# Two modulation vectors of each FFN phase as row sums on the vector engine, and six raw buffers instead of seven

## The chip, the cores and the metric

One core of a Trainium2 chip runs the kernel. The metric is the device time of one execution in microseconds (us). Times within one execution are counted from the first instruction of its profile. A change of 0.2% of this kernel is 2.75 us.

## What is computed

The reference is a trunk of two layers. Each layer is run for 128 context tokens and 128 latent tokens with the same weights. A layer has three parts (a gated FFN, a token mixer, a second gated FFN), and each part is modulated by a shift, a scale and a gate that come from the conditioning vector of the token group:

```python
def modulate(x, shift, scale):
    return x * (1 + scale[:, None, :]) + shift[:, None, :]
def adaln(cvec, w, b):                        # w: (1024, 9 * 1024), b: (9 * 1024,)
    m = jax.nn.silu(cvec) @ w + b
    return jnp.split(m, N_MOD, axis=-1)
...
    sh1, sc1, gt1, sh2, sc2, gt2, sh3, sc3, gt3 = mods
    u = modulate(rms_norm(x, g[0]), sh1, sc1)
    x = x + 0.5 * gt1[:, None, :] * swiglu(u, lp['w_ffn1_in'], lp['w_ffn1_out'])
    u = modulate(rms_norm(x, g[1]), sh2, sc2)
    y, ctx_out = token_mixer(u, lp, lam_init, ctx)
    x = x + gt2[:, None, :] * y
    u = modulate(rms_norm(x, g[2]), sh3, sc3)
    x = x + 0.5 * gt3[:, None, :] * swiglu(u, lp['w_ffn2_in'], lp['w_ffn2_out'])
```

`adaln` gives nine vectors of 1024 values for each layer and for each of two conditioning vectors. Each of the nine reads a 1024 x 1024 slice of `w_ada`, 4 MB in float32. `DEPTH` is 2, so there are 18 such vectors; vector (l, m) is number m of layer l.

## The kernel before, in words

All weights come from HBM in float32 and are used once. A weight chunk (`Chunk`, mostly 1 MB, 8 KB in each partition) is loaded by the SP queue into one of `N_RAW` = 7 buffers named `raw` (L1466 to L1471). Its products need float32 accuracy, so each half of a chunk (a `Unit`) is split by `split_one` into a rounded part `whi` (scalar engine, L1493) and a remainder `wlo` (vector engine, L1494). `mm3` (L167) then multiplies three pairs of parts on the tensor engine: high by high (L168), high by low (L169) and low by high (L170). Six split units may wait for the tensor engine (`N_SPLIT`). A raw buffer is given back when the last reader of its chunk is through, and `pump_dma` then lets SP issue the next chunk of one fixed list. That list is sorted by need: a chunk that is split is due six units ahead of its products, a chunk that is read as it is stands at its own step.

The program is a list of steps, worked off in order by the executor at the end of the file; each engine sees its own instructions in that order. An FFN's first part has eleven column pairs of four units (24 matmuls each), its second part has 24 units. The FFN phases begin at 0, 507, 708 and 1175 us, and their first parts end at about 175, 645, 845 and 1305 us. The mixers lie between them.

The modulation vectors that a later part needs are worked out as extra steps, which `spread_into` puts evenly between the steps of a phase. `ADA` says which vectors each phase works out, and in which of two ways:

- A vector of the second list takes four 1 MB chunks of `w_ada`, two at a time in one step. `side` (L310) runs 16 instructions of the tensor engine with 512 columns for two chunks: four products side by side, each with 32 columns of `cT` as the stationary operand (`pd<-raw,cT`, L165). So a vector is two steps.
- A vector of the first list is first summed over its eight channel blocks on the vector engine: 28 of 32 instructions multiply a 128 x 512 block by one value per partition and add it to `acc` (L339), the others begin the sum (L337). Then `total` sums the 128 lanes of `acc` on the tensor engine with the constant `hot` (`pd<-acc,hot`), twice for each vector.

At the end of a phase `post` transposes the gathered sums, adds the two halves and the bias, and finishes scale and gate vectors.

Three FFN phases have one vector of the first kind and two of the second, the last FFN phase has one of the first kind. The mixers have three of the second kind each. The first two vectors, (0, 0) and (0, 1), belong to `begin`, the opening of the kernel, in which each 1 MB chunk of `w_ada` gives one channel block (L1343 to L1403). `begin` ends with `last` and then `s_loads` (L257), which loads some small inputs over the POOL queue; the step list of the first phase has its modulation steps from its 20th step on.

Of the kernel before, what the change touches and what calls it, by code (L numbers as in the profile page):

```python
# [17 lines left out]
P = 128  # L18
# [15 lines left out]
N_RAW = 7  # L34
# [5 lines left out]
HOT = 10  # L40
LAG = 2
# modulation vectors that each phase works out: those the vector engine sums first, and the others
ADA = {(0, "ffn1"): ([(0, 4)], [(0, 2), (0, 3)]),
       (0, "mixer"): ([], [(0, 7), (0, 6), (0, 5)]),
       (0, "ffn2"): ([(1, 1)], [(0, 8), (1, 0)]),
       (1, "ffn1"): ([(1, 4)], [(1, 2), (1, 3)]),
# [33 lines left out]
def _pack(inputs):  # L80
    """Short vectors side by side, 128 wide, and the per-head gate biases and stabilisers."""
# [43 lines left out]
def trunk_kernel(ctx: ExitStack, tc: tile.TileContext, a: dict):  # L125
# [18 lines left out]
    def t2(shape, name, dt=F32):  # L144
        return tp.tile(shape, dt, tag="t2", name=name, bufs=N_T2)
# [38 lines left out]
    # ---------------------------------------------------------------- small inputs  # L184
# [15 lines left out]
    hot = const.tile([P, HOT + 32], F32, name="hot")  # L200
    po.memset(hot, 0.0)
    po.memset(hot[:, HOT:HOT + 1], 1.0)
# [4 lines left out]
    # ---------------------------------------------------------------- persistent  # L207
# [9 lines left out]
    identb = const.tile([P, P], BF16, name="identb")  # L217
    maskb = const.tile([P, 2, P], BF16, name="maskb")
# [25 lines left out]
    # ---------------------------------------------------------------- start-up  # L244
# [12 lines left out]
    def s_loads():  # L257
        late_in["msk"] = t2([P, 2, P], "msk")
        late_in["lamp"] = t2([P, DEPTH, 4, 64], "lamp")
        po.dma_start(out=late_in["lamp"], in_=a["attn_lambda"].partition_broadcast(P))  # L260
        po.dma_start(out=cst[:, C_CS:C_MF], in_=a["cst"][:, C_CS:C_MF])
        po.dma_start(out=late_in["msk"], in_=a["cst"][:, C_MF:C_END].rearrange("p (d t) -> p d t", d=2))
# [35 lines left out]
    # ---------------------------------------------------------------- modulation  # L298
    def mod_steps(mods_):
        """Products of some modulation vectors.  # L300

        Four products run side by side: two quarters of the channels, two terms of their sums.
        Vector i takes the rows 2 i and 2 i + 1 of each. The vector engine first sums the channel
        blocks of those of the first list, one term per group, and the products sum its lanes."""
        on_ve, on_pe = mods_
        n_ve, mods_ = len(on_ve), on_ve + on_pe
        st = {"left": 4 * len(on_pe) + 2 * n_ve}
# [12 lines left out]

        for i, (l, m) in enumerate(on_ve):
            for r in range(2):
                acc = []
                for jj in range(2):
                    f0 = m * D + r * 512
                    ch = Chunk(a["w_ada"][l, jj * 512:(jj + 1) * 512, f0:f0 + 512], 4, 512)
                    for e in range(4):
                        u = Unit(ch, e, e + 1, 0, 512, split=False)

                        def fn(u=u, k=4 * jj + e, acc=acc):  # L330
                            w = u.raw()[:, 0, :]
                            if k == 0:
                                acc.append(blk([P, 2, 512], "acc"))
                            for g in range(2):
                                c, x = cT[:, k, CT + g:CT + g + 1], acc[0][:, g, :]
                                if k == 0:
                                    ve.tensor_scalar(x, w, c, None, op0=ALU.mult)  # L337
                                else:
                                    ve.scalar_tensor_tensor(x, w, c, x, op0=ALU.mult, op1=ALU.add)  # L339

                        seq.append(((2 * i + r) * 8 + 4 * jj + e + 0.5, fn, [u]))

                def total(i=i, r=r, acc=acc):
                    side([(hot[:, HOT - 2 * i - g:HOT - 2 * i - g + 32], acc[0][:, g, c * 256:c * 256 + 256])
                          for g in range(2) for c in range(2)], r * 256, r * 256 + 256)

                seq.append(((2 * i + r) * 8 + 7.5 + LAG, total, []))
        span = 16 * n_ve if n_ve else 1
        for i, (l, m) in enumerate(on_pe):
            for j2 in range(2):  # L350
# [5 lines left out]
                def fn(us=us, i=n_ve + i, j2=j2):  # L356
# [5 lines left out]
                seq.append(((4 * i + 2 * j2 + 0.4) * span / (4 * len(on_pe)), fn, us))  # L362
        seq.sort(key=lambda x: x[0])
        out = [x[1:] for x in seq]

        def post():
# [12 lines left out]
            for i, (l, m) in enumerate(mods_):  # L379
                o, x = mods[l, m], full[:, :, 2 * i:2 * i + 2]  # L380
                bT = parT[l][:, m * KD:(m + 1) * KD].unsqueeze(2).to_broadcast([P, KD, 2])
                ve.tensor_add(o, x, bT)
                if m % 3 == 1:
                    k0 = 72 + m // 3 * KD
# [1175 lines left out]
```

## Time and profile before

| | us |
|---|---|
| three runs | 1376.32, 1376.99, 1379.35 |
| median of the runs | 1376.99 |
| the profiled execution, first to last instruction | 1375.88 |
| tensor engine (PE) busy in it | 1351.3 (98%) |
| vector engine (DVE) busy | 915.0 (67%) |
| scalar engine (ACT) busy | 682.3 (50%) |
| moved by DMA | 303.68 MB |

The profile is of one execution. Its record runs from the first to the last instruction, and that span, 1375.88 us, is the only time that the record has of it; it lies 1.1 us under the median of the runs. "Busy" is the time in which at least one instruction of the engine runs. An engine's weight loads (PEld) overlap its matmuls.

### The profile page before, as it was taken

How to read it: one execution, taken by the hardware profiler on the slowest of the kernel's cores; microseconds unless marked ns; L12 is line 12 of the kernel's file. 1: busy time of each engine (PE TensorE's matmuls, PEld its weight loads, DVE VectorE, ACT ScalarE, POOL GpSimd, SP SyncE). 2: the span in 40 equal slices, each digit the busy share in tenths (PEclk: the TensorE clock that was granted, in tenths of full speed). 3: DMA queues.
4: the chain of work that ended last, by engine and by line, in shares of the span. 5: the costliest groups of instructions: out<-in, count | busy, mean ns of one | idle time of the engine just before them, and what ended most of it. 6: DMA issues, size and time to landing. Idle time of an engine off the chain costs nothing.

```text
span 1375.9 us, 26101 instructions
## 1 busy us (share of the span) xinstructions
PE 1351.3 (98%) x10915; PEld 1268.7 (92%) x10916; DVE 915.0 (67%) x1440; ACT 682.3 (50%) x1096; POOL 113.0 (8%) x138
## 2 busy tenths in 40 slices
PE   6999999999999999999999999999999999999998
PEld 4999899888998999999998999998899899999998
DVE  4576755876557589666568666667665668887653
ACT  4544444666544466444455444546564445744442
POOL 2000001300000030000020000130000001200000
PEclk8999999999999999999999999999999999999999
DMA  9999856564468847886639876748445895487520
GB/s 293 333 345 340 260 174 213 159 195 138 157 238 298 272 154 267 300 269 212 206 124 321 305 257 197 204 130 241 154 137 195 297 304 186 147 264 233 192 85 31
DMA packets 247526, 303.68 MB, mean 221 GB/s; under 512 B 5537, under 2 KB 212657, under 8 KB 247409
## 3 DMA queue, kind: packets, MB, share of 16 engines
q1 hardware_dynamic: 245728, 296.98, 66.4%
q0 software_dynamic: 1680, 5.05, 1.1%
q8 instruction: 85, 1.39, 0.4%
q14 instruction: 33, 0.26, 0.1%
HBM read 297.80 MB, written 3.15 MB: 219 GB/s over the span
## 4 chain that ended last, share of the span: by engine, by line
PE 90%; DVE 6%; ACT 2%; DMA 1%; issue 1%; SPq 1%; POOL 0%; ACTq 0%; DVEq 0%
PE pm L168 26%; PE pm L170 25%; PE pm L169 25%; PE pd L165 5%; PE pb L165 2%; DVE wlo L1494 2%; DVE v L498 2%; DVE ul L180 1%; PE pm L752 1%; PE pm L754 1%; PE pm L753 1%; ACT whi L1493 1%; PE pa L165 1%; DMA raw<-w_ada 1%; PE pa L173 1%
## 5 line engine op out<-in xcount | busy, mean ns | idle before, releaser
L1494 DVE TENSOR_TENSOR wlo<-raw,whi 128x1024 fp32r<-128x1024 f32 (+1 forms) x424 | 507.3, 1204 | 326.4 <-ACT whi L1493 316.8
L1493 ACT CAST whi<-raw 128x1024 fp32r<-128x1024 f32 (+1 forms) x424 | 433.9, 1031 | 364.3 <-PE pm L169 253.4
L168 PE MATMUL pm<-uh,whi 128*128 128x256 f32 x1928 | 554.7, 288 | 0.0
L169 PE MATMUL pm<-ul,whi 128*128 128x256 f32 x1928 | 546.8, 284 | 1.7 <-DVE v L498 1.3
L170 PE MATMUL pm<-uh,wlo 128*128 128x256 f32 x1928 | 544.7, 283 | 3.2 <-DVE wlo L1494 3.2
L168 PEld LDWEIGHTS pm<-uh,whi 128*128 128x128 f32 x1928 | 366.8, 190 | 23.7 <-ACT whi L1493 9.1
L170 PEld LDWEIGHTS pm<-uh,wlo 128*128 128x128 f32 x1928 | 366.4, 190 | 4.4 <-DVE wlo L1494 4.4
L169 PEld LDWEIGHTS pm<-ul,whi 128*128 128x128 f32 x1928 | 366.2, 190 | 3.8 <-DVE v L498 1.7
L169 PE MATMUL pm<-hl,whi 128*128 128x256 f32 x704 | 197.9, 281 | 0.0
L168 PE MATMUL pm<-hh,whi 128*128 128x256 f32 x704 | 197.5, 281 | 0.0
L170 PE MATMUL pm<-hh,wlo 128*128 128x256 f32 x704 | 197.5, 281 | 0.0
L168 PEld LDWEIGHTS pm<-hh,whi 128*128 128x128 f32 x704 | 132.8, 189 | 0.0
L170 PEld LDWEIGHTS pm<-hh,wlo 128*128 128x128 f32 x704 | 132.7, 189 | 0.0
L169 PEld LDWEIGHTS pm<-hl,whi 128*128 128x128 f32 x704 | 132.6, 188 | 0.0
L423 POOL TENSOR_TENSOR nsum<-nsum,nsq 128x256 f32<-128x256 f32 x36 | 36.4, 1012 | 833.7 <-ACT nsq L421 833.7
L339 DVE SCALAR_TENSOR_TENSOR acc<-raw,cT,acc 128x512 f32<-128x512 f32 x112 | 78.9, 746 | 0.0
L165 PE MATMUL pd<-raw,cT 128*32 128x512 f32 (+1 forms) x512 | 56.5, 560 | 8.7 <-DMA raw<-w_ada 5.0
L653 ACT ACTIVATE silu<-pm 128x512 f32<-128x512 f32 x39 | 23.3, 597 | 69.5 <-PE pm L170 69.5
L165 PEld LDWEIGHTS pd<-raw,cT 128*32 128x32 f32 x512 | 14.0, 112 | 30.8 <-issue 20.4
L655 DVE TENSOR_TENSOR silu<-silu,pm 128x512 f32<-128x512 f32 x40 | 27.4, 685 | 22.6 <-PE pm L170 22.6
L568 DVE SCALAR_TENSOR_TENSOR xT<-pm,mod,xT 128x128 f32<-128x128 f32 x96 | 28.8, 342 | 18.1 <-PE pm L170 18.0
L1238 ACT ACTIVATE sig<-pm 128x512 f32<-128x512 f32 x24 | 14.4, 598 | 50.3 <-PE pm L170 50.1
(340 smaller groups left out, 1757.8 us busy)
## 6 DMA issues: line engine op xcount, KB each, us to landing
raw<-w_ffn_in SPq DMA_DIRECT2D x88, 1024.0 KB, 7.1
raw<-w_ada SPq DMA_DIRECT2D x64, 1024.0 KB, 6.0
raw<-w_ffn_out SPq DMA_DIRECT2D x32, 1024.0 KB, 7.1
raw<-w_in SPq DMA_DIRECT2D x32, 1024.0 KB, 5.9
raw<-w_branch_gate SPq DMA_DIRECT2D x24, 1024.0 KB, 5.4
raw<-w_ffn_out SPq DMA_DIRECT2D x16, 768.0 KB, 4.8
raw<-w_ada SPq DMA_DIRECT2D x16, 512.0 KB, 7.3
raw<-w_out SPq DMA_DIRECT2D x8, 1024.0 KB, 6.6
```

Source lines behind the costliest of these rows:

```text
L165: pe.matmul(out, lhsT, rhs, start=start, stop=stop)
L168: pe.matmul(out, sh, mh, start=start, stop=False)
L169: pe.matmul(out, sh, ml, start=False, stop=False)
L170: pe.matmul(out, sl, mh, start=False, stop=stop)
L339: ve.scalar_tensor_tensor(x, w, c, x, op0=ALU.mult, op1=ALU.add)
L423: eng.tensor_add(self.sum, self.sum, sq)
L498: ve.tensor_scalar(v[:, G[1]], v[:, G[1]], self.scale[:, k, 1:2], self.shift[:, k, 1:2], op0=ALU.mult, op1=ALU.add)
L568: ve.scalar_tensor_tensor(xT[:, k, G[g]], ps[:, G[g]], gate[:, k, g:g + 1], xT[:, k, G[g]], op0=ALU.mult, op1=ALU.add)
L653: ac.activation(st["s"], st["a"], AF.Silu)
L655: ve.tensor_mul(st["s"], st["s"], st["g"])
L1493: ac.copy(u.hi, r)
L1494: ve.tensor_sub(u.lo, r, u.hi.bitcast(F32))
```

## The change

The vectors of the first list are worked out in another way, one more vector of three phases moves to that list, and one raw buffer goes.

```diff
-N_RAW = 7
+N_RAW = 6
...
-ADA = {(0, "ffn1"): ([(0, 4)], [(0, 2), (0, 3)]),
+ADA = {(0, "ffn1"): ([(0, 4), (0, 3)], [(0, 2)]),
        (0, "mixer"): ([], [(0, 7), (0, 6), (0, 5)]),
-       (0, "ffn2"): ([(1, 1)], [(0, 8), (1, 0)]),
-       (1, "ffn1"): ([(1, 4)], [(1, 2), (1, 3)]),
+       (0, "ffn2"): ([(1, 1), (1, 0)], [(0, 8)]),
+       (1, "ffn1"): ([(1, 4), (1, 3)], [(1, 2)]),
        (1, "mixer"): ([], [(1, 7), (1, 6), (1, 5)]),
        (1, "ffn2"): ([(1, 8)], [])}
...
+    cb = const.tile([P, 2, D], F32, name="cb")
...
     def s_loads():
...
+        po.dma_start(out=cb, in_=a["cc"].partition_broadcast(P))
+        ac.activation(cb, cb, AF.Silu)
         po.dma_start(out=late_in["lamp"], in_=a["attn_lambda"].partition_broadcast(P))
...
         for i, (l, m) in enumerate(on_ve):
-            for r in range(2):
...
-                                if k == 0:
-                                    ve.tensor_scalar(x, w, c, None, op0=ALU.mult)
-                                else:
-                                    ve.scalar_tensor_tensor(x, w, c, x, op0=ALU.mult, op1=ALU.add)
...
-                def total(i=i, r=r, acc=acc):
-                    side([(hot[:, HOT - 2 * i - g:HOT - 2 * i - g + 32], acc[0][:, g, c * 256:c * 256 + 256])
-                          for g in range(2) for c in range(2)], r * 256, r * 256 + 256)
...
+            o, junk = mods[l, m], []
+            for j in range(KD // 2):
+                ch = Chunk(a["w_adaT"][l, m, j], 2, D)
+                for b in range(2):
+                    for g in range(2):
+                        u = Unit(ch, b, b + 1, 0, D, split=False)
+
+                        def fn(u=u, k=2 * j + b, g=g, o=o, l=l, m=m, junk=junk):
+                            if not junk:
+                                junk.append(blk([P, D], "junkw"))
+                            ve.tensor_tensor_reduce(junk[0], u.raw()[:, 0, :], cb[:, g, :], 1.0, 0.0,
+                                                    op0=ALU.mult, op1=ALU.add, accum_out=o[:, k, g:g + 1])
+                            if k == KD - 1 and g == 1:
+                                finish(l, m, o, o)
+
+                        seq.append(((i + (4 * j + 2 * b + g) / 16) / len(on_ve), fn, [u]))
...
+        if not mods_:
+            return out
...
+    arrays["cc"] = np.stack([inputs["c_ctx"], inputs["c"][0]])
+    wt = inputs["w_ada"].reshape(DEPTH, D, N_MOD, KD // 2, 2, P)
+    arrays["w_adaT"] = np.ascontiguousarray(wt.transpose(0, 2, 3, 5, 4, 1))
```

`w_adaT` is `w_ada` with its output channels along the partitions and its 1024 input channels in a row, two blocks of 128 output channels to a 1 MB chunk, 8 KB in one piece for each partition. The host lays it out. `cb` is the SiLU of both conditioning vectors, the same 2 x 1024 values in every partition (1 MB in all, as large as the raw buffer that goes). One `tensor_tensor_reduce` multiplies a 128 x 1024 block by one of the two vectors and writes the sum of each row, which is the modulation value of that output channel. So a vector of the first list is 16 steps of one vector-engine instruction each, with no product and no `total`; `finish` is the old end of `post` as a function of its own. Where the second list is empty, `post` is left out. The constant `hot` and its memsets are gone.

## Rows read from the trace of the kernel before

**Rows 1.** The page: engine totals, forty equal slices, and the chain that ended last.

```profile
PE 1351.3 (98%) x10915; PEld 1268.7 (92%) x10916; DVE 915.0 (67%) x1440; ACT 682.3 (50%) x1096; POOL 113.0 (8%) x138
...
PE   6999999999999999999999999999999999999998
...
PEclk8999999999999999999999999999999999999999
DMA  9999856564468847886639876748445895487520
...
PE 90%; DVE 6%; ACT 2%; DMA 1%; issue 1%; SPq 1%; POOL 0%; ACTq 0%; DVEq 0%
```

**Rows 2.** Stretches: start:end, length, busy of each engine (instructions), clock, DMA share, GB/s.

```profile
10.00:50.00 40.00, 31.29 (x256) 21.98 (x256) 18.88 (x46) 15.37 (x29) 9.81 (x11) 0.83 1.13 311
80.00:172.00 92.00, 91.21 (x764) 83.27 (x763) 65.03 (x84) 39.81 (x46) 0.00 (x0) 1.00 0.91 307
519.00:644.00 125.00, 124.24 (x1044) 116.47 (x1043) 90.29 (x123) 59.20 (x76) 0.00 (x0) 1.00 0.84 277
1188.00:1305.00 117.00, 116.24 (x984) 114.68 (x983) 89.69 (x121) 59.33 (x76) 0.00 (x0) 1.00 0.69 225
```

**Rows 3.** PE by line: the first three of 519 to 644 us, the last of 80 to 172.

```profile
L165 PE MATMUL pd<-raw,cT 128*32 128x512 f32 x64 | 7.7, 598 | 0.0
L165 PE MATMUL pd<-acc,hot 128*32 128x256 f32 x16 | 1.3, 391 | 0.0
L173 PE MATMUL pd<-cst,adaev 128*128 128x128 f32 x4 | 0.6, 272 | 0.0
...
L165 PE MATMUL pd<-acc,hot 128*32 128x256 f32 x16 | 1.9, 391 | 0.8 <-DVE acc L339 0.8
```

**Rows 4.** DVE by line, 519 to 644 us: busy, mean ns of one, idle before.

```profile
L1494 DVE TENSOR_TENSOR wlo<-raw,whi 128x1024 fp32r<-128x1024 f32 (+1 forms) x44 | 53.0, 1216 | 28.6 <-ACT whi L1493 27.5 <-PE pd L165 1.1
L339 DVE SCALAR_TENSOR_TENSOR acc<-raw,cT,acc 128x512 f32<-128x512 f32 x28 | 19.7, 745 | 0.0
L655 DVE TENSOR_TENSOR silu<-silu,pm 128x512 f32<-128x512 f32 x9 | 6.2, 685 | 5.0 <-PE pm L170 5.0
L337 DVE TENSOR_SCALAR acc<-raw,cT 128x512 f32<-128x512 f32 x4 | 1.8, 482 | 0.0
```

**Rows 5.** Other shapes, whole span, by form: a smaller DVE instruction, the scalar engine's accumulator.

```profile
L865 DVE SCALAR_TENSOR_TENSOR pl<-e,cf,pl 128x256 f32<-128x256 f32 x8 | 3.5, 481 | 0.1
...
L856 ACT ACTIVATION_READ_ACCUMULATOR e<-pa,mx 128x1 f32 x16 | 3.6, 228 | 0.0
```

**Rows 6.** POOL in order of time, 0 to 60 us, the issue of lamp and what precedes it.

```profile
12.84 7.39 POOL L1394 TENSOR_TENSOR v<-xT,bcs 128x256 f32<-128x256 f32 x7 [1.85 <-ACT bcs L486]
44.73 0.63 POOL L260 DMA_DIRECT2D lamp<-attn_lambda  x1 [24.50 <-PE pd L173]
```

**Rows 7.** Who waited for whom, 0 to 60 us: total, times, longest.

```profile
PE pd L165 <- DMA raw<-w_ada: 5.0, 3, 3.5
```

**Rows 8.** The scalar engine in order of time, 52 to 70 us.

```profile
55.98 3.88 ACT L1493 CAST whi<-raw 128x1024 fp32r<-128x1024 f32 x4
...
60.38 2.00 ACT L1493 CAST whi<-raw 128x1024 fp32r<-128x1024 f32 x2
```

**Rows 9.** SP's own waits over the whole span.

```profile
SPq L1471 <- DVE wlo L1494: 864.1, 166, 21.1
```

**Rows 10.** SP issues by time, 519 to 580 us, then the product that reads the pair.

```profile
561.05 6.61 SPq L1471 DMA_DIRECT2D raw<-w_ada  x2
572.43 7.65 SPq L1471 DMA_DIRECT2D raw<-w_ffn_in  x4
...
578.59 1.50 PE L165 MATMUL pd<-raw,cT 128*32 128x512 f32 x12
```

**Rows 11.** DMA issues: KB each, median us to landing; whole span, then 519 to 644.

```profile
raw<-w_ada SPq DMA_DIRECT2D x64, 1024.0 KB, 6.0
...
raw<-w_ada SPq DMA_DIRECT2D x9, 1024.0 KB, 8.5
```

More of the change, by code (lines that the diff above doesn't have):

```diff
@@ L39 @@
 CT = 8
-HOT = 10
-LAG = 2
-ADA = {(0, "ffn1"): ([(0, 4)], [(0, 2), (0, 3)]),
+ADA = {(0, "ffn1"): ([(0, 4), (0, 3)], [(0, 2)]),
        (0, "mixer"): ([], [(0, 7), (0, 6), (0, 5)]),
-       (0, "ffn2"): ([(1, 1)], [(0, 8), (1, 0)]),
-       (1, "ffn1"): ([(1, 4)], [(1, 2), (1, 3)]),
+       (0, "ffn2"): ([(1, 1), (1, 0)], [(0, 8)]),
+       (1, "ffn1"): ([(1, 4), (1, 3)], [(1, 2)]),
        (1, "mixer"): ([], [(1, 7), (1, 6), (1, 5)]),
@@ L199, in trunk_kernel @@
     po.memset(expo, -0.5)
-    hot = const.tile([P, HOT + 32], F32, name="hot")
-    po.memset(hot, 0.0)
-    po.memset(hot[:, HOT:HOT + 1], 1.0)
     cT = const.tile([P, KD, CT + 32], F32, name="cT")
@@ L299, in mod_steps @@
     def mod_steps(mods_):
-        on_ve, on_pe = mods_
-        n_ve, mods_ = len(on_ve), on_ve + on_pe
-        st = {"left": 4 * len(on_pe) + 2 * n_ve}
+        on_ve, mods_ = mods_
+        st = {"left": 4 * len(mods_)}
         seq = []
@@ L319, in side @@
                 ac.copy(st["ev"], st["ps"])
-        for i, (l, m) in enumerate(on_ve):
-            for r in range(2):
[L323 to L331, printed above, removed]
-                            if k == 0:
[L333 to L336, printed above, removed]
-                                    ve.tensor_scalar(x, w, c, None, op0=ALU.mult)
-                                else:
-                                    ve.scalar_tensor_tensor(x, w, c, x, op0=ALU.mult, op1=ALU.add)
-                        seq.append(((2 * i + r) * 8 + 4 * jj + e + 0.5, fn, [u]))
-                def total(i=i, r=r, acc=acc):
-                    side([(hot[:, HOT - 2 * i - g:HOT - 2 * i - g + 32], acc[0][:, g, c * 256:c * 256 + 256])
-                          for g in range(2) for c in range(2)], r * 256, r * 256 + 256)
-                seq.append(((2 * i + r) * 8 + 7.5 + LAG, total, []))
@@ L348, in mod_steps, with finish @@
-        span = 16 * n_ve if n_ve else 1
-        for i, (l, m) in enumerate(on_pe):
+        def finish(l, m, o, x):
+            bT = parT[l][:, m * KD:(m + 1) * KD].unsqueeze(2).to_broadcast([P, KD, 2])
+            ve.tensor_add(o, x, bT)
+            if m % 3 == 1:
+                k0 = 72 + m // 3 * KD
+                gT = parT[l][:, k0:k0 + KD].unsqueeze(2).to_broadcast([P, KD, 2])
+                ve.scalar_tensor_tensor(o, o, 1.0, gT, op0=ALU.add, op1=ALU.mult)
+            elif m % 3 == 2 and m != 5:
+                ve.tensor_scalar(o, o, 0.5, None, op0=ALU.mult)
@@ L350, in mod_steps @@
+        for i, (l, m) in enumerate(mods_):
             for j2 in range(2):
@@ L354, in mod_steps, with fn @@
                     us.append(Unit(ch, 0, 2, 0, D, split=False))
-                def fn(us=us, i=n_ve + i, j2=j2):
+                def fn(us=us, i=i, j2=j2):
                     for j, u in enumerate(us, 2 * j2):
@@ L360, in fn @@
                               for e in range(2) for c in range(2)], 0, 512)
-                seq.append(((4 * i + 2 * j2 + 0.4) * span / (4 * len(on_pe)), fn, us))
+                seq.append(((2 * i + j2 + 0.4) / (2 * len(mods_)), fn, us))
         seq.sort(key=lambda x: x[0])
         out = [x[1:] for x in seq]
+        if not mods_:
+            return out
         def post():
@@ L379, in post @@
             for i, (l, m) in enumerate(mods_):
[L380 to L384, printed above, removed]
-                    gT = parT[l][:, k0:k0 + KD].unsqueeze(2).to_broadcast([P, KD, 2])
-                    ve.scalar_tensor_tensor(o, o, 1.0, gT, op0=ALU.add, op1=ALU.mult)
-                elif m % 3 == 2 and m != 5:
-                    ve.tensor_scalar(o, o, 0.5, None, op0=ALU.mult)
+                finish(l, m, mods[l, m], full[:, :, 2 * i:2 * i + 2])
         out.append((post, []))
@@ L1470, in pump_dma @@
             else:
-                nc.sync.dma_start(out=t, in_=c.src.rearrange("(k p) f -> p k f", p=P))
+                src = c.src if len(c.src.shape) == 3 else c.src.rearrange("(k p) f -> p k f", p=P)
+                nc.sync.dma_start(out=t, in_=src)
             c.tile = t
```

## The prediction

> **What bounds the kernel now.** I read the page first [rows 1]. The tensor engine is busy 98% of the span, all slices but the first and the last are full, its clock is granted nearly everywhere, and the chain that ended last runs through it for 90%. The vector engine has a third of its time free. So an instruction that leaves the tensor engine should shorten the run by its own length, unless something else then ends last. What that could be I read from stretches [rows 2]. From 10 to 50 us, in `begin`, the tensor engine is busy 31.29 of 40 us and the DMA engines are saturated (share 1.13, 311 GB/s): the start is bound by loading. In the first phase's modulation stretch (80 to 172 us) the tensor engine is full, DMA stands at 0.91 and the vector engine at 65.03 of 92 us. In the second FFN phase (519 to 644) DMA is at 0.84, the vector engine at 90.29 of 125; the third repeats it. The last (1188 to 1305) has DMA at 0.69.
>
> **What the change takes from the tensor engine.** In one FFN phase the two vectors of the second list are 64 instructions, 7.7 us together, 3.85 us for each vector [rows 3]. A second price: the stretches 519 to 644 and 1188 to 1305 do the same FFN work with and without two such vectors, and differ by 124.24 - 116.24 = 8.0 us of tensor time [rows 2], 4.0 us for each, with what switching costs. I take 4.0. Three vectors move: 12.0 us. `total` goes in all four phases, 1.3 us in each [rows 3] (in the first the row reads 1.9 because its group is stretched by a wait of 0.8 us for `acc`, which goes too): 5.2 + 0.8 us. In the last phase `post`'s four transposes go: 0.6 us [rows 3]. Sum: 12.0 + 5.2 + 0.8 + 0.6 = **18.6 us**.
>
> **What it puts on the vector engine.** No row shows a `tensor_tensor_reduce`. By the nearest rows: a plain two-input 128x1024 instruction (`wlo`) takes 1.22 us, or 53.0 / 44 = 1.20 us of busy time [rows 4]. `scalar_tensor_tensor` takes 745 ns for 512 columns and 481 ns for 256 [rows 4, 5], so 1.03 ns a column, and 745 + 528 = 1273 ns for 1024. Neighbours overlap a little: 28 of them fill 19.7 us, 0.70 us each and not 0.745 [rows 4], which makes it 1.23 us. Writing the row sum may cost nothing or, as on the scalar engine, an instruction of its own of up to 0.23 us [rows 5]. Bounds 1.2 and 1.46 us; I take 1.3, since the form is nearest to `scalar_tensor_tensor`.
>
> [...]
>
> In the second and third FFN phases the vector engine gives back 19.7 + 1.8 = 21.5 us [rows 4] and gets 32 x 1.3 = 41.6: 90.3 - 21.5 + 41.6 = 110.4 us in a stretch that shrinks to 125 - 8/2 - 1.3 = 119.7 us. It fits, at 92%. In the first phase the same 32 instructions lie in the shorter stretch: 65.0 - 21.5 + 41.6 = 85.1 us in 92 - 4.0 - 1.3 - 0.8 = 85.9 us, 99%. The cover here is the stock of six split units (six times 24 matmuls, some 17 us of products) and the gated products' PSUM tiles (three tiles, which let the vector engine fall four units, about 11 us, behind). The waits for `whi` that the vector engine now has (27.5 us in the second phase [rows 4]) are idle time ahead of a full stock and go first. At 1.46 us the first phase wants 90.2 us: 4.3 us late, inside that cover. The last phase trades 21.5 us for 20.8. So I cost the vector engine at nothing.
>
> **What it adds elsewhere.** (a) `cb` is one more megabyte. Its issue stands in `s_loads`, but on POOL's queue it is next after the seven multiplications that end at 12.84 + 7.39 = 20.2 us; what follows there now, `lamp`, waits 24.5 us for a buffer of its own [rows 6], and `cb`, being a constant tile, needs none. So it lands in the middle of the saturated start, where products already wait for chunks of `w_ada` (5.0 us in three waits [rows 7]). 1.05 MB at 311 GB/s is 3.4 us [rows 2]. Bounds: 0 (hidden behind the other waits of the start) and 3.4; I take 3.4, as the chunks behind it are used as they land. The SiLU of 128 x 2048 on the scalar engine, about twice the 1.04 us of a 1024-column cast, stands at about 60 us between casts [rows 8] that run six units ahead; `cb` has then long landed, so nothing waits. If the cover failed it would cost 2.1 us once.
>
> (b) Six raw buffers. SP waits 864 us in all for a raw buffer that `wlo` frees [rows 9], so the buffers are full most of the time and each issue moves to the next release. In the second FFN phase the second chunk of a pair for the tensor engine is issued at about 567.3, the next release is at 572.4, and the pair is used at 578.6 [rows 10]. Issued at 572.4 it lands at 578.4 by the whole span's median of 6.0 us, or at 580.9 by this stretch's 8.5 [rows 11]: a wait of 0 to 2.3 us for each pair. Six such pairs remain in the FFN phases (twelve before), with fewer loads bunched around them; the mixers' pairs have more room. Bounds 0 and 13.8 us; I take 1.0.
>
> (c) The first phase's loading. 307 GB/s over 92 us is 28.2 MB; at a full share (307 / 0.91 = 337 GB/s) that takes 83.8 us, and the tensor engine will want it in 85.9. DMA is then at 98%, with one buffer fewer to smooth it. Bounds 0 (it keeps up) and 6.1 us (the phase stays as long as it is); I take half, 3.0. The new chunks come in 8 KB pieces instead of 2 and 4 KB, which no row here prices; I give it nothing.
>
> **Sum.** -18.6 + 3.4 + 1.0 + 3.0 = -11.2 us against the span of 1375.9 us; with 1.1 us outside it the median was 1377.0, so I predict **1366 us**. With every added cost at 0 it is 1358.4.
>
> **The rivals.**
>
> 1. *Loading takes most of it.* The start costs 3.4, the first phase gains nothing (6.1), and each pair elsewhere waits 1 us (6): -18.6 + 15.5 = -3.1, 1374 us. For it: share 1.13 at the start and 0.91 after. Against it: the second and third phases load at 0.84 and the last at 0.69 [rows 2].
>
> 2. *Six buffers are too few: slower.* As rival 1, but every pair waits the full 2.3 us: -18.6 + 3.4 + 6.1 + 13.8 = +4.7, 1382 us. The place is `pd<-raw,cT` in the FFN phases, where the tensor engine stands still with its own queue behind it. It turns slower once a pair waits over (18.6 - 9.5) / 6 = 1.5 us. Against it: only half as many pairs are left there.
>
> [...]
>
> 4. *Nothing to measure*, within 0.2% (2.75 us, about what a measurement of this kernel tells from no change): the upper half of rival 1 or the lower edge of rival 2.
>
> **How the numbers follow.** My forecast, 1357 to 1371 us: 0.64. Rival 1 (1371 to 1377): 0.18, two thirds of it still over 0.2% faster. Rival 2: 0.10. Rival 3: 0.07. Over: 0.01. So faster 0.64 + 0.12 = 0.76, the same 0.06 + 0.02 = 0.08, slower 0.16. The range reaches from every added cost at nothing, 1357, to the end of rival 1, 1377.
>
> **What would show it.** Right: `pd<-raw,cT` falls from 64 to 32 instructions in each of three FFN phases and `pd<-acc,hot` is gone; the row sum reads 1.2 to 1.46 us; the stretch of the second FFN phase ends some 5 us sooner after its start; the first chunks of `w_ada` land about 3 us later. Wrong: a row sum of 2 us or more, with idle tensor time released by `wlo` or by the gated products' tiles in the FFN phases; or idle tensor time before `pd<-raw,cT`, released by DMA. If the start is not longer, (a) was hidden; if the first phase is shorter by the full 6 us, (c) was.

## The result: 1361.2 us, 15.4 us less, and the profile after

| | before | after |
|---|---|---|
| median of the runs, us | 1376.65 (4 runs) | 1361.21 (4 runs, 1359.85 to 1361.61) |
| ratio to before, 95% interval | | 0.9889 [0.9875, 0.9904] |
| profiled execution, first to last instruction, us | 1375.9 | 1358.1 |
| PE / DVE busy in it, us | 1351.3 / 915.0 | 1328.9 / 959.8 |

The forecast was 1366 us. The kernel got faster by 15.4 us between the medians and by 17.8 us between the two profiled executions, and both lie beyond the 11.2 us of the sum. The page of the kernel after, with the lines that answer to [rows 1]:

```profile
PE 1328.9 (98%) x10752; PEld 1258.0 (93%) x10752; DVE 959.8 (71%) x1533; ACT 683.0 (50%) x1096; POOL 113.4 (8%) x137
...
PE   6999999999999999999999999999999999999998
...
DMA  9999966563578846987538987648445895477630
...
PE 84%; DVE 8%; DMA 3%; ACT 2%; issue 1%; SPq 0%; POOL 0%; DVEq 0%; ACTq 0%
```

The tensor engine still sets the time: 98% busy, but 22.4 us less of it. 44.8 us more stand on the vector engine, and the slices between the ends show no gap. The stretches that answer to [rows 2], shifted to where the phases now lie (columns as there):

```profile
10.00:50.00 40.00, 30.51 (x234) 20.82 (x235) 17.45 (x40) 14.05 (x26) 9.05 (x10) 0.79 1.10 312
80.00:172.00 92.00, 92.00 (x777) 88.86 (x776) 84.08 (x128) 44.05 (x51) 0.00 (x0) 1.00 0.91 309
512.00:633.00 121.00, 119.40 (x1002) 115.53 (x1000) 106.09 (x156) 59.34 (x77) 0.00 (x0) 1.00 0.85 286
1172.00:1288.00 116.00, 115.25 (x975) 114.66 (x975) 88.77 (x121) 60.25 (x78) 0.07 (x1) 1.00 0.70 228
```

In the first phase's stretch the tensor engine doesn't stand still at all (92.00 of 92.00 us), although DMA is at 0.91 as before and the vector engine has gone from 65 to 84 us. In the second FFN phase the vector engine is busy 106.1 of 121 us (88%).

The second FFN phase by line, first the vector engine (answers to [rows 4]), then the tensor engine (answers to [rows 3]):

```profile
L1485 DVE TENSOR_TENSOR wlo<-raw,whi 128x1024 fp32r<-128x1024 f32 (+1 forms) x44 | 53.3, 1216 | 8.8 <-ACT whi L1484 8.8
L339 DVE CUSTOM_DVE_ANT_0 junkw<-raw,cb 128x1024 f32<-128x1024 f32 x32 | 39.0, 1219 | 0.0
...
L339 DVE DVE_READ_ACCUMULATOR2_ANT mod<- 128x1 f32 x32 | 2.7, 83 | 0.0
```

```profile
L163 PE MATMUL pd<-raw,cT 128*32 128x512 f32 x32 | 4.1, 601 | 0.8 <-DMA raw<-w_ada 0.8
```

A row sum is two instructions on the vector engine, of 1219 ns for the multiplication and 83 ns for reading the accumulator. They are not to be added, because they overlap. In order of time (two row sums that follow each other at the end):

```profile
96.50 1.22 DVE L339 CUSTOM_DVE_ANT_0 junkw<-raw,cb 128x1024 f32<-128x1024 f32 x1
97.65 0.08 DVE L339 DVE_READ_ACCUMULATOR2_ANT mod<- 128x1 f32 x1
97.65 1.22 DVE L1485 TENSOR_TENSOR wlo<-raw,whi 128x1024 fp32r<-128x1024 f32 x1
...
102.21 1.22 DVE L339 CUSTOM_DVE_ANT_0 junkw<-raw,cb 128x1024 f32<-128x1024 f32 x1
...
103.47 1.23 DVE L339 CUSTOM_DVE_ANT_0 junkw<-raw,cb 128x1024 f32<-128x1024 f32 x1
```

Another instruction starts 1.15 us behind the start of a row sum, a second row sum 1.26 us behind it. The busy time of both instructions of L339 together, in the second FFN phase, is 39.25 us for 32 row sums, 1.23 us each:

```profile
512.00:633.00 121.00, 39.25 (x64) 1.00 0.85 286
```

`pd<-raw,cT` has gone from 64 to 32 instructions and `pd<-acc,hot` is gone. The vector engine's idle time ahead of `whi` has gone from 27.5 to 8.8 us: the row sums took the place of waiting.

**Where the 17.8 us went.** I cut both profiled executions at the same products, found in order of time: the first product of each FFN's first part (`pm<-uh,whi`) and of its second part (`pm<-hh,whi`), rounded to 0.1 us. Two of these cuts are the first `uh` product of the second phase, before and after:

```profile
519.00 0.28 PE L168 MATMUL pm<-uh,whi 128*128 128x256 f32 x1
```

```profile
512.03 0.28 PE L166 MATMUL pm<-uh,whi 128*128 128x256 f32 x1
```

| stretch | before, us | after, us | difference | by the sum |
|---|---|---|---|---|
| start, to the products of the eighth `w_ada` chunk | 49.0 | 50.9 | +1.9 | +3.4 |
| from there to the second part of the first FFN | 126.2 | 119.1 | -7.1 | -6.1 + 3.0 |
| second part, and the first mixer | 343.8 | 342.0 | -1.8 | 0 |
| first part of the second FFN | 125.3 | 120.6 | -4.7 | -5.3 |
| its second part | 75.7 | 75.9 | +0.2 | 0 |
| first part of the third FFN | 124.7 | 120.4 | -4.3 | -5.3 |
| its second part, and the second mixer | 343.1 | 343.5 | +0.4 | 0 |
| first part of the last FFN | 116.8 | 114.4 | -2.4 | -1.9 |
| the rest | 71.3 | 71.3 | 0 | 0 |

The sum's 1.0 us for six buffers has no row of its own; it belongs to the first parts. The -1.8 of the first mixer is the clock's: the stretch lies behind an opening, where the tensor engine has short waits, and in the profiled execution of before its clock then fell (stretches of it: columns as in [rows 2], the clock before the last two):

```profile
250.00:254.00 4.00, 3.29 (x25) 2.71 (x23) 3.54 (x7) 2.20 (x7) 4.00 (x6) 1.00 0.44 132
254.00:258.00 4.00, 3.39 (x13) 2.37 (x14) 2.98 (x5) 3.40 (x5) 1.21 (x4) 0.72 0.42 130
258.00:262.00 4.00, 4.00 (x21) 4.00 (x21) 3.89 (x13) 1.21 (x3) 0.00 (x0) 0.50 0.91 258
```

The same place in the execution of after:

```profile
245.00:249.00 4.00, 3.31 (x24) 2.73 (x22) 3.54 (x8) 2.01 (x6) 4.00 (x6) 1.00 0.56 149
249.00:253.00 4.00, 3.10 (x18) 2.14 (x17) 2.98 (x6) 3.25 (x4) 0.88 (x4) 1.00 0.33 114
253.00:257.00 4.00, 4.00 (x35) 3.94 (x34) 3.86 (x14) 1.40 (x4) 0.00 (x0) 1.00 0.97 291
```

After 3.3 and 3.4 busy microseconds of four the clock stands at 0.50, for 21 instructions in 4 us; with 3.3 and 3.1 it stayed at 1.00, for 35. It isn't the change's: a kernel with the engines' work of after (4 KB pieces, below) shows 0.96 from 225 to 310 us where after shows 1.00, takes 344.0 us for the second part and the first mixer, has a span of 1360.3 us, and the same median. Without the 1.8 us the profiled executions differ by 16.0 us, near the 15.4 of the medians.

### The profile page after: what moved, and what is told of

Its sections match the earlier page's. It is cut to its first block, busy times and chain, and to the rows that moved or that the text cites. A ratio compares the mean times of both kernels' runs of the same rounds, so it can differ in the third digit from the quotient of the medians.

```text
span 1358.1 us, 25895 instructions
## 1 busy us (share of the span) xinstructions
PE 1328.9 (98%) x10752; PEld 1258.0 (93%) x10752; DVE 959.8 (71%) x1533; ACT 683.0 (50%) x1096; POOL 113.4 (8%) x137
## 4 chain that ended last, share of the span: by engine, by line
PE 84%; DVE 8%; DMA 3%; ACT 2%; issue 1%; SPq 0%; POOL 0%; DVEq 0%; ACTq 0%
PE pm L166 25%; PE pm L167 24%; PE pm L168 24%; PE pd L163 3%; DVE wlo L1485 3%; PE pb L163 2%; DMA raw<-w_ada 2%; DVE v L488 2%; ACT whi L1484 1%; DVE ul L178 1%; PE pm L742 1%; PE pm L743 1%; PE pm L744 1%; PE pa L163 1%; DVE junkw L339 1%
## 5 line engine op out<-in xcount | busy, mean ns | idle before, releaser
L166 PEld LDWEIGHTS pm<-uh,whi 128*128 128x128 f32 x1928 | 364.4, 189 | 15.8 <-ACT whi L1484 7.7
L339 DVE CUSTOM_DVE_ANT_0 junkw<-raw,cb 128x1024 f32<-128x1024 f32 x112 | 136.5, 1219 | 0.1
L163 PE MATMUL pd<-raw,cT 128*32 128x512 f32 (+1 forms) x416 | 46.0, 559 | 11.4 <-DMA raw<-w_ada 9.6
L177 ACT CAST hh<-silu 128x512 fp32r<-128x512 f32 (+1 forms) x42 | 25.5, 609 | 32.7 <-DVE silu L645 32.7
L1228 ACT ACTIVATE sig<-pm 128x512 f32<-128x512 f32 x24 | 14.3, 598 | 50.2 <-PE pm L168 50.1
L742 PE MATMUL pm<-whi,uh 128*128 128x512 f32 x96 | 39.3, 409 | 0.0
```

Of the source, the lines that this page charges most:

```text
L163: pe.matmul(out, lhsT, rhs, start=start, stop=stop)
L166: pe.matmul(out, sh, mh, start=start, stop=False)
L177: ac.copy(hi, src)
L339: ve.tensor_tensor_reduce(junk[0], u.raw()[:, 0, :], cb[:, g, :], 1.0, 0.0, op0=ALU.mult, op1=ALU.add, accum_out=o[:, k, g:g + 1])
L742: pe.matmul(ps[g], xh[:, G[g]], wh, start=(k == 0), stop=False)
```

## The experiments

Times are medians beside runs of the kernel before on the same chip; ratios are to the kernel before. A ratio is known to some 0.001 to 0.002, which is 1.4 to 2.8 us, so a difference of 3 us between two changed kernels is near what the medians can tell. Stretches are cut as in the table above.

### One part alone: the row sums without a third vector

```diff
-ADA = {(0, "ffn1"): ([(0, 4), (0, 3)], [(0, 2)]),
+ADA = {(0, "ffn1"): ([(0, 4)], [(0, 2), (0, 3)]),
...
-       (0, "ffn2"): ([(1, 1), (1, 0)], [(0, 8)]),
-       (1, "ffn1"): ([(1, 4), (1, 3)], [(1, 2)]),
+       (0, "ffn2"): ([(1, 1)], [(0, 8), (1, 0)]),
+       (1, "ffn1"): ([(1, 4)], [(1, 2), (1, 3)]),
```

> The changed kernel with the lists of the kernel before: one vector of an FFN phase as row sums, two as products. Against the kernel before it takes only the lane totals and the last transposes from the tensor engine (6.6 us) and pays for cb (2 to 3.4 us) and the buffer (1 to 2). My theory (the gain is the tensor work of the three moved vectors): 1372 to 1375 us, some 12 us over the changed kernel. Rival (the gain comes from how the vector engine's vectors are loaded and summed, in longer pieces and with half the instructions): within 3 us of the changed kernel, 1361 to 1364.

1372.45 us, 0.9968 [0.9956, 0.9980], inside the theory's range and far from the rival's. The four phases' stretches of the table are 123.1, 123.7, 123.4 and 114.3 us, so against before the new form by itself (no `total`, in the last phase no transposes) gave 3.1, 1.6, 1.3 and 2.5 us: 8.5, where the sum had 6.6. Against the kernel after, a moved vector is worth 4.0, 3.1 and 3.0 us: 10.1, where the sum had 12.0. Together 18.6 us, the sum's figure, but that is luck: the new form gave 1.9 us more than the sum had, the moved vectors 1.9 less.

The kernel after waits for `w_ada` once in the second and once in the third FFN phase (510 to 640 and 710 to 840 us):

```profile
PE pd L163 <- DMA raw<-w_ada: 0.8, 1, 0.8
```

```profile
PE pd L163 <- DMA raw<-w_ada: 0.7, 1, 0.7
```

With one row-sum vector and the same six buffers there is no such wait in these two phases. So 1.5 of the 1.9 us by which the moved vectors fell short are these waits.

### One part alone: six raw buffers in the kernel before

```diff
-N_RAW = 7
+N_RAW = 6
```

> The kernel before with six raw buffers instead of seven and nothing else. It keeps all twelve pairs of w_ada chunks in the FFN phases, so it is the harder case for a missing buffer. My theory (the buffer costs a short wait at a pair here and there): 0 to 3 us longer, so 1377 to 1380 us, with waits for w_ada in the trace of at most 1 us each. Rival 2 of the prediction (each pair waits some 2.3 us, and the loading of the first phase falls behind): 12 x 2.3 = 28 us and up to 6 more, so 1400 us or over.

1380.86 us, 1.0033 [1.0023, 1.0044]: the seventh buffer is worth 4.3 us there, a little over my theory's 0 to 3 and far from the rival's 28. The tensor engine's waits from 510 to 640 and from 710 to 850 us, each view's first line:

```profile
PE pd L165 <- DMA raw<-w_ada: 2.0, 1, 2.0
```

```profile
PE pd L165 <- DMA raw<-w_ada: 0.9, 1, 0.9
```

With seven buffers there is no such wait in these phases. The waits stand where the sum put them, at the pairs of chunks for the tensor engine, in the second and third FFN phases, whose first parts took 127.5 and 125.7 us (before: 125.3 and 124.7). One of the two is longer than the 1 us that I had expected at most. The first FFN's stretch stayed at 126.2 us and loads as much as before:

```profile
80.00:172.00 92.00, 91.21 (x765) 83.26 (x764) 65.08 (x85) 39.83 (x46) 0.00 (x0) 1.00 0.89 297
```

So one buffer fewer costs nothing in the phase in which I had feared for the loading.

### The megabyte of `cb` later

```diff
-        po.dma_start(out=cb, in_=a["cc"].partition_broadcast(P))
-        ac.activation(cb, cb, AF.Silu)
...
+        po.dma_start(out=cb, in_=a["cc"].partition_broadcast(P))
...
+            if jj == 3 and l == 0 and which == 1:
+                add(lambda: ac.activation(cb, cb, AF.Silu))
```

The load goes behind the last small input of `s_loads`, the SiLU into a step of its own after `begin`, and the first row sum one step later.

> The changed kernel with the load of cb behind the other small loads on the POOL queue (at about 51 us instead of 21) and its SiLU just ahead of the first row sum. My theory (the megabyte lengthens the saturated start by about its own length): 2 to 3.4 us shorter than the changed kernel, 1358 to 1359 us, and the eighth chunk of w_ada is multiplied at about 48 us instead of 50.9. Rival (the start has slack for it): the same as the changed kernel, 1361 us. Second rival (the first phase, with DMA at 0.91, is tighter than the start): up to 3 us longer, 1364 us.

1357.88 us, 0.9859 [0.9842, 0.9876], 3.3 us less than the kernel after. The issue on POOL, in the kernel after and in this one:

```profile
21.04 0.63 POOL L256 DMA_DIRECT2D cb<-cc  x1
46.55 0.56 POOL L258 DMA_DIRECT2D lamp<-attn_lambda  x1 [24.88 <-PE pd L171]
```

```profile
48.38 0.53 POOL L259 DMA_DIRECT2D cb<-cc  x1
```

Each with a product of the start that waits for `w_ada`, after and here:

```profile
34.35 1.93 PE L163 MATMUL pd<-raw,cT 128*32 128x256 f32 x16 [5.16 <-DMA raw<-w_ada]
```

```profile
31.49 1.93 PE L163 MATMUL pd<-raw,cT 128*32 128x256 f32 x16 [4.04 <-DMA raw<-w_ada]
```

`cb` does go out at 21 us, right behind POOL's multiplications, into the saturated start (DMA share 1.10 from 10 to 50 us), and the same product comes 2.9 us sooner without it. It is so in every profiled execution here: this product starts at 33.9 to 34.4 us in the seven with the early load, and at 31.4 to 31.8 us in the six without it. Term (a), 3.4 us, is thus seen as 3.3 us between the medians and as 2.2 us at the eighth chunk's products of these two executions (50.9 and 48.7 us), and it was avoidable. The first phase's stretch stayed at 119.0 us with `cb`'s load in it, so the second rival's tight first phase did not show.

### The pieces of a load: 4 KB instead of 8 KB

```diff
-                ch = Chunk(a["w_adaT"][l, m, j], 2, D)
+                ch = Chunk(a["w_adaT"][l, m, j].rearrange("b p f -> p b f"), 2, D)
...
-    arrays["w_adaT"] = np.ascontiguousarray(wt.transpose(0, 2, 3, 5, 4, 1))
+    arrays["w_adaT"] = np.ascontiguousarray(wt.transpose(0, 2, 3, 4, 5, 1))
```

> The changed kernel with w_adaT laid out so that each partition's 8 KB of a chunk comes in two pieces of 4 KB that lie apart, as the chunks of the products have it, instead of one. Nothing else differs. My prediction gave the longer pieces nothing: then the same as the changed kernel, 1360 to 1362 us. Rival (the longer pieces are why the first phase kept up with its loading): 1 to 3 us longer, in the first phase, with a longer time to landing for w_adaT.

1361.28 us, 0.9886 [0.9869, 0.9902], against 1361.21. The larger pieces give nothing, as the sum had it.

### The row sums twice: how much cover is there

```diff
                             ve.tensor_tensor_reduce(junk[0], u.raw()[:, 0, :], cb[:, g, :], 1.0, 0.0,
                                                     op0=ALU.mult, op1=ALU.add, accum_out=o[:, k, g:g + 1])
+                            ve.tensor_tensor_reduce(junk[0], u.raw()[:, 0, :], cb[:, g, :], 1.0, 0.0,
+                                                    op0=ALU.mult, op1=ALU.add, accum_out=o[:, k, g:g + 1])
```

Each row sum is worked out a second time into the same place, so that at the prediction's 1.3 us it takes 2.6 us of the vector engine.

> [...] By the prediction's working (11 us of cover in each phase): the first phase 126.7 us of vector work in 85.9, 30 late, the second and third 152.0 in 119.7, 21 late each, the last fits: about 72 us longer than the changed kernel, 1433 us. If the vector engine were no bound until much later, or the cover larger (the 17 us of split units), it would be 18 us less, about 1415; if there were no cover at all, 33 more, 1466.

1422.17 us, 1.0329 [1.0312, 1.0345], 61 us over the kernel after, where I had 72. It shows what a vector engine costs that wants twice the time for its row sums. The first phase's stretch took 139.1 us, 20.0 more, and the second and third phases 17.3 and 18.0 more. Its page, a stretch of the first phase, and the whole first part of the second:

```profile
PE 1345.0 (95%) x10752; PEld 1269.8 (90%) x10752; DVE 1093.5 (77%) x1757; ACT 674.9 (48%) x1096; POOL 113.3 (8%) x137
```

```profile
80.00:172.00 92.00, 79.56 (x637) 74.54 (x636) 90.69 (x141) 31.70 (x38) 0.00 (x0) 0.94 0.71 242
535.68:673.60 137.92, 124.27 (x999) 117.19 (x997) 135.39 (x204) 55.44 (x74) 0.00 (x0) 0.95 0.70 235
```

How far the vector engine may fall behind at no cost, its cover, comes out of this. By the prediction's own busy times it wants 85.1 + 41.6 = 126.7 us in the 85.9 of the first phase, 40.8 too many; 20.0 appeared, which leaves 20.8 us of cover, and in the second phase 110.4 + 41.6 - 119.7 - 17.3 = 15.0. But those busy times are too high. The 112 extra row sums added 1093.5 - 959.8 = 133.7 us, 1.19 us each and 38.2 for the 32 of a phase. With the busy times measured in the kernel after, the first phase has 84.1 + 38.2 - 92 - 20.0 = 10.3 us of cover and the second 106.1 + 38.2 - 121 - 17.3 = 6.0. That is an estimate. It lies nearer to the 11 us of the PSUM tiles with which I had worked out the 72 than to the 17 us of the six split units; which of the two stocks makes the cover wasn't tested. In the trace the last row sum ends 11.1 and 5.8 us after the second part's first product, in the kernel after 2.0 and 5.3 us before it.

The tensor engine's longest waits from 510 to 680 us:

```profile
PE pd L163 <- DMA raw<-w_ada: 11.4, 4, 5.4
PE pm L166 <- DVE silu L647: 1.5, 1, 1.5
```

The vector engine is the one that is short of time, 135.4 of 137.9 us, and yet the longest line names DMA, while DMA's share is 0.70 where the kernel after has 0.85. The longest of these four waits is for a load that was issued late (SP's issue, then the product that reads the chunk):

```profile
562.02 0.37 SPq L1464 DMA_DIRECT2D raw<-w_ada  x1
...
567.17 1.08 PE L163 MATMUL pd<-raw,cT 128*32 128x512 f32 x4 [5.39 <-DMA raw<-w_ada]
```

SP issued this load when a row sum (`mod`, L341) had given its raw buffer back, it landed at 567.13, and the product started 0.04 us later. The row sum is a chunk's last reader, a late vector engine gives the buffer back late, and SP has nowhere to load to. Whoever reads the first line alone blames the wrong thing.

### Three vectors in three phases: where the vector engine becomes the bound

```diff
+ADA = {(0, "ffn1"): ([(0, 4), (0, 3), (0, 2)], []),
...
+       (0, "ffn2"): ([(1, 1), (1, 0), (0, 8)], []),
+       (1, "ffn1"): ([(1, 4), (1, 3), (1, 2)], []),
```

> The changed kernel with all three vectors of an FFN phase as row sums, which leaves the tensor engine no modulation work there. It takes 12 us of products, 2 us of transposes and some 2 us of waits from it, and puts 16 x 1.30 = 20.8 us more on the vector engine of three phases: 106.1 + 20.8 = 126.9 us in about 116 in the second and third, 84.1 + 20.8 = 104.9 in about 87 in the first. My theory (the stock of split units and the PSUM tiles let it fall 11 us behind at no cost): only the first phase is late, by 7 us, so 9 us shorter than the changed kernel, about 1352 us. Rival (what does not fit is lost at once): 10.6 + 10.6 + 18 us late, so about 1384 us.

1355.60 us, 0.9849 [0.9835, 0.9862]: 5.6 us less than the kernel after, so the rival's loss did not come, but also not all of the gain. The first parts of the second and third phases became shorter by 6.6 and 6.7 us (114.0, 113.7), and the first whole phase longer by 2.9 (236.0 against 233.1). In the first phase's stretch the vector engine is full and the tensor engine isn't; in the second phase both are:

```profile
80.00:172.00 92.00, 87.61 (x734) 86.89 (x733) 90.05 (x137) 36.82 (x45) 0.00 (x0) 1.00 0.79 271
517.60:631.60 114.00, 114.00 (x963) 114.00 (x962) 112.25 (x165) 52.46 (x69) 0.00 (x0) 1.00 0.80 271
```

And the phase began later. From the end of the phase before to the first `uh` product it took 14.3 and 15.8 us in the second and third phase, where the kernel after takes 12.5 and 12.5. The vector engine at the opening of the second phase, in order of time, here:

```profile
503.22 1.57 DVE L339 CUSTOM_DVE_ANT_0 junkw<-raw,cb 128x1024 f32<-128x1024 f32 x1
504.72 0.08 DVE L339 DVE_READ_ACCUMULATOR2_ANT mod<- 128x1 f32 x1
504.78 2.36 DVE L1485 TENSOR_TENSOR wlo<-raw,whi 128x1024 fp32r<-128x1024 f32 x2
507.06 0.15 DVE L463 TENSOR_SCALAR var<-pb 128x2 f32<-128x2 f32 x1
```

With an empty second list the first row sum falls due ahead of the phase's first own step, and two splits follow it. `var`, with which the norm of the phase goes on, comes at 507.06, 3.8 us after the residual's end at 503.3; in the kernel after it comes 1.6 us behind it (501.13 against 499.5):

```profile
501.13 0.16 DVE L463 TENSOR_SCALAR var<-pb 128x2 f32<-128x2 f32 x1 [1.62 <-PE pb L163]
```

The tensor engine waits there for the norm, in both phases about 2.1 us; in the second:

```profile
508.51 0.68 PE L163 MATMUL pb<-dg,ones 128*128 128x256 f32 x2 [2.09 <-ACT dg L470]
```

In the third phase its clock fell behind that wait (0.64 over 4 us), which is the larger part of what makes 3.3 us there of the 1.8 in the second:

```profile
702.00:706.00 4.00, 4.00 (x25) 4.00 (x24) 3.96 (x6) 2.99 (x8) 3.80 (x5) 0.64 0.23 94
```

In a phase the row sums have cover (10.3 and 6.0 us by the estimate above); at its opening they had none (2.1 us of waiting).

### The same in two phases, one step later

```diff
-        spread_into(p0 + (21 if begun else 0), p1, mods_)
+        spread_into(p0 + (21 if begun else 1), p1, mods_)
```

With the later `cb`, and three row-sum vectors in the second and third phase alone.

> cb loaded late (1357.9 us), three vectors as row sums in the second and third FFN phase, two in the first, and the first row sum of the second to fourth FFN phase one step later, behind the norm's step and not ahead of it. In three_rowsum the first products of the second and third phase took 6.7 us less than in the changed kernel (114.1 and 113.8 us against 120.8 and 120.6), but they began 1.8 and 3.3 us later after the phase before. My theory (the vector engine's 11 us of cover hold, and the late start came from the row sum that stood ahead of the norm): 2 x 6.7 less, 1344 to 1347 us. Rival (the late start is the price of the fuller vector engine wherever the row sums stand): 5 us more, 1349 to 1351.

1350.09 us, 0.9815 [0.9801, 0.9830], 7.8 us less than with the later `cb` alone; that is the rival's figure and not the theory's. The delay at the openings is gone (12.6 and 12.5 us), but the first parts take 115.0 us each, where three vectors in all three phases had 114.0 and 113.7. The only wait of the tensor engine in this stretch is one of 0.8 us for `wlo`, which the kernel after has too and that run lacks. The vector engine is all but full:

```profile
514.00:630.00 116.00, 115.24 (x970) 114.97 (x971) 114.90 (x168) 53.35 (x69) 0.00 (x0) 1.00 0.82 280
```

114.9 of 116 us: a third vector is what these phases still hold. Its last row sum ends 9.3 us after the second part's first product, so the phase already leans on its cover. A fourth wasn't tried.

### Single chunks, and five buffers

The pairs of chunks for the tensor engine were the place where I had looked for waits. This loads and uses them one at a time:

```diff
-            for j2 in range(2):
+            step = 1 if on_ve else 2
+            for j2 in range(4 // step):
...
-                for j in range(2 * j2, 2 * j2 + 2):
+                for j in range(step * j2, step * j2 + step):
```

> The changed kernel with the products of an FFN phase's one vector taken one w_ada chunk at a time, in four steps spread over the phase instead of two steps of two chunks. The number of chunks, products and row sums is the same. My theory (with six buffers a step that needs two landed chunks at once waits for the second): the waits of the tensor engine for w_ada in the second and third FFN phase (some 1 to 1.7 us in each) go, 1.5 to 3 us shorter than the changed kernel, 1358 to 1360 us. Rival (the wait is the saturated loading itself, whatever the order): no shorter, 1361 us or more.

1361.50 us, 0.9890 [0.9876, 0.9905]: no gain. The two waits of the kernel after, of 0.8 and 0.7 us, are gone here. Whether twice as many steps cost what the wait gave back isn't told apart.

```diff
-N_RAW = 6
+N_RAW = 5
```

> The changed kernel with five raw buffers instead of six. [...] In the kernel before the seventh was worth 4.3 us (raw6), all of it in the second and third FFN phase. My theory (with half of the pairs gone the changed kernel has room at six and is past it at five): 3 to 8 us longer, 1364 to 1369 us, as waits for w_ada at the remaining pairs. Rival (the buffers no longer matter to it): within 1.5 us of 1361.

1374.80 us, 0.9993 [0.9984, 1.0001], 13.6 us more than the kernel after and more than either side expected. The waits of the second phase (510 to 640 us) against the 0.8 us of the kernel after:

```profile
PE pd L163 <- DMA raw<-w_ada: 4.0, 3, 2.2
```

Five buffers take nearly the whole gain back. The first FFN phase got 1.5 us longer, the first parts of the second and third 5.0 and 5.1. Over the whole span the tensor engine waits 21.0 us for `w_ada`, in the kernel after 9.6. The clock took a share: it is 0.97 from 540 to 600 us, where after has 1.00. What a seventh buffer beside `cb` would give in the changed kernel wasn't tried.

### A row-sum vector in each mixer, and all together

With the later `cb`:

```diff
-       (0, "mixer"): ([], [(0, 7), (0, 6), (0, 5)]),
+       (0, "mixer"): ([(0, 6)], [(0, 7), (0, 5)]),
...
-       (1, "mixer"): ([], [(1, 7), (1, 6), (1, 5)]),
+       (1, "mixer"): ([(1, 6)], [(1, 7), (1, 5)]),
```

> The changed kernel with cb loaded late (as in cb_late, 1357.9 us) and one of the three vectors of each mixer moved to row sums as well. It takes 2 x 4 us of products from the tensor engine and puts 20.8 us on the vector engine of each mixer, which is 63% busy in the stretch where these steps lie. My theory (a vector moved is worth its products wherever the vector engine has room): 6 to 8 us shorter than cb_late, 1350 to 1352 us. Rival (the mixers' many short steps on the vector engine end late behind the row sums, or their scratch tile takes a block that the mixer needs): no shorter, 1358 us or more.

1351.09 us, 0.9821 [0.9802, 0.9841]: 6.8 us less for two vectors, 3.4 each, as the theory had it. From 380 to 460 us, in the first mixer, the tensor engine is busy in all 80 us and the vector engine in 67.4, so there is room there too.

> three_in_two with one vector of each mixer as row sums as well, as in mixer_cb (which was 6.8 us shorter than cb_late). My theory (the stretches are independent, since each is bound by its own tensor work): the gains add up, 1337 to 1341 us. Rival (with seven vectors of a layer on it the vector engine starts each phase late from the one before): less than half of the mixers' gain is left, 1342 us or more.

Later `cb`, three row-sum vectors in the second and third FFN phases, and one in each mixer: **1340.78 us, 0.9750 [0.9737, 0.9764]**, 20.4 us less than the kernel after and the fastest of all. That is 9.3 us less than without the mixers' vectors, inside the theory's range, so the gains add up. Its page shows how far the exchange has gone:

```profile
PE 1311.4 (98%) x10615; PEld 1256.2 (94%) x10616; DVE 1028.9 (77%) x1655; ACT 676.2 (51%) x1094; POOL 113.0 (8%) x137
```

## Why the prediction was right, and where it was off

**Right: what bounds the kernel, and the direction.** What leaves the tensor engine leaves the time. The removed work was put at 18.6 us and measured at 8.5 + 10.1 = 18.6, but that the two agree is luck. A moved vector gave the 4.0 us that I took for it in the first phase, but 3.1 and 3.0 in the second and third, where the 0.8 and 0.7 us of waits for `w_ada` take the difference but for some 0.3 us. The new form alone gave 1.9 us more than the 6.6 of the sum, 1.0 of it in the first phase. There I had misread the last line of [rows 3]: its 1.9 us are busy time and the 0.8 us of waiting come on top, 2.7 together, where I had put 2.1. The rest I didn't separate.

**Nearly right: the vector engine's price.** Taken 1.3 us, between bounds of 1.2 and 1.46; measured 1.23 of busy time. The 32 of a phase keep the engine busy for 39.25 us against 41.6. The two records add up to 1.30, but that is no confirmation, since they overlap. Writing the sum is an instruction of its own, which I had held possible, and takes 83 ns where the scalar engine's took 228 ns [rows 5]. With two float32 SBUF sources and an accumulator, the 1219 ns of the multiplication are those of the plain two-input instruction beside it (1216 ns). The profile names it `CUSTOM_DVE_ANT_0`.

**Right, but hardly tested by the change: the cover.** The vector engine was costed at nothing and cost nothing that shows: no wait of the tensor engine in the first phase's stretch. But it was busy for 84 of 92 us there, 91%, where I had reckoned with 99%, so it had little need of cover. By the doubled row sums and measured busy times the cover is some 6 to 10 us, where I had 17 and 11.

**Right: (a), the start.** 3.4 us predicted, 3.3 us by the medians with the later load, which know it to 2 or 3 us. In the profiled executions the start shows 1.9 us more than before and 2.2 us more than with the later load (48.7 us).

**Wrong: (c), the first phase's loading.** I took 3.0 us between bounds of 0 and 6.1; the stretch gave 7.1 us, the whole of the 6.1 and 1.0 more. The step that failed is the working from 28.2 MB and a full share of 337 GB/s to a share of 98%. Its ceiling was too low. The kernel before itself loads faster, just ahead of that window and with the tensor engine busy throughout:

```profile
50.00:80.00 30.00, 30.00 (x255) 29.88 (x252) 20.48 (x26) 19.07 (x27) 0.00 (x0) 1.00 1.07 363
```

At 363 GB/s the 28.2 MB take 77.7 us, well inside 85.9. And it takes all that is loaded in the window for what the window needs. The loads of 80 to 172 us in the kernel before were these (KB each, median us to landing):

```profile
raw<-w_ada SPq DMA_DIRECT2D x9, 1024.0 KB, 8.8
raw<-w_ffn_in SPq DMA_DIRECT2D x9, 1024.0 KB, 8.1
raw<-w_ffn_out SPq DMA_DIRECT2D x6, 1024.0 KB, 7.8
raw<-w_ffn_out SPq DMA_DIRECT2D x2, 768.0 KB, 4.9
```

Six and two of them, 6 x 1.05 + 2 x 0.79 = 7.9 MB, are `w_ffn_out`, which the second part reads from 175 us on. So part of the load is stock for later. How much of it could wait wasn't tested: by the start of the second part the kernel after has issued eight such chunks and the kernel before nine. The kernel after loads at the same 0.91 share, moves 26.5 MB from 84 to 170 us, and has no wait of the tensor engine in the stretch. A high DMA share in a stretch was no proof that the stretch waits for loading; the waits for a load were, and there were none.

**About right: (b), six buffers.** Taken 1.0 us, between bounds of 0 and 13.8; the waits at the pairs are 0.8 and 0.7 us, 1.5 together, one in each of two phases and none in the first. They are inside the 10.1 us of the moved vectors already, so the measured -18.6 and `cb`'s 3.3 make -15.3, near the -15.4, without a term for them. The mechanism is real, and steep: 4.3 us from seven to six in the kernel before, 13.6 from six to five in the kernel after, with single waits for `w_ada` of up to 2.2 us in these phases.

So the 4.2 us between the sum (-11.2) and the measurement (-15.4) are 3.0 of (c) and 1.5 of removed work that the sum had too small (18.6 + 1.5 = 20.1 without the waits), less the 0.5 by which (b) was too small; 0.1 is (a), and 0.1 is lost in rounding. Rivals 1, 2 and 4 fell with the waits that did not come; the 0.07 of rival 3 were for a row-sum instruction long enough to make the kernel slower (some 2 us, by the prediction's busy times and its 11 us of cover), which no run shows: the runs showed 1219 ns, 1.23 us of busy time. What too full a vector engine costs is seen in the doubled row sums: the prediction's busy times and its 11 us of cover give 29.8 in the first phase and 21.3 in each of the next two, 72 us, and 61 were measured. With measured busy times and the same 11 us they are 19.3 and 12.3 in the first and second phase, against 20.0 and 17.3 measured: the price was too high, and in the second phase the cover was too high as well.

## What to carry to other kernels

Where one engine is full and another has idle time that is waiting ahead of a full stock, work can be moved to the second, here until it was busy for 114.9 of 116 us, as long as it isn't put where the first engine waits for the second: at the opening of a phase one row sum and two splits ahead of the norm cost 1.8 and 3.3 us. Add up busy time and not the lengths of records, which overlap (1219 and 83 ns for 1.23 us). Judge loading by waits for loads; before taking a DMA share for a bound (0.91 here, with no wait), look for a faster stretch in the same trace and ask for which stretch a loaded megabyte is meant. A new constant's load belongs behind the saturated start: one megabyte issued 27 us later was worth 3.3 us by the medians and 2.2 by the profiled start.

## What the runs showed of the hardware beyond that

- A `tensor_tensor_reduce` of 128 x 1024 float32 values from two SBUF sources is 1219 ns and an accumulator read of 83 ns, which starts some 75 ns before its end. In the lines shown above the next instruction started 1.15 us behind the start of a row sum when it was another one, and 1.26 us behind it when it was a row sum again.
- The same instruction took 1.57 us at 503.2 us in one run's phase opening, against a mean of 1.22, and 1.21 at the next phase's opening; what slowed it there wasn't tested.
- Behind the opening of the first mixer the clock fell to 0.50 in the profiled execution of before and stayed at 1.00 in that of after, with nearly the same idle time ahead of it (1.3 and 1.6 of 8 us). From 225 to 310 us it is 0.96 in six of the thirteen profiled executions, 0.98 in four and 1.00 in three: the 1.8 us belong to neither kernel.
